# Gate and up tiles of a feed-forward in pairs by seven quarter products, with five feed-forward parts

## The chip, the cores and the metric

The kernel runs on one core of one Trainium2 chip. The metric is the device time of one execution in microseconds (us). Three runs of the kernel before gave 2639.88, 2640.99 and 2644.07 us, a median of 2640.99 us.

## The reference

One inference step of a two-layer hybrid trunk (width 1024) for 128 prompt tokens and 512 sample tokens, which share the weights. Each layer computes

```
h = rmsnorm(x) * (1 + scale1) + shift1
z = h @ w_in                        # conv, attention and S5 inputs, three gates
merged = sum_i sigmoid(g_i) * (y_i @ w_proj_i)
x += gate1 * (merged @ w_out)
h = rmsnorm(x) * (1 + scale2) + shift2
x += gate2 * ((silu(h @ w_ffn_gate) * (h @ w_ffn_up)) @ w_ffn_down)
```

The feed-forward width is 2816. All inputs are float32, and the result is compared at float32 accuracy.

## The kernel before

Channels lie on the 128 partitions and all 640 tokens along the free axis, so one pass over the weights serves both groups. Every operand of a large product is split exactly into two float32r parts (`split`, L255: ACT writes hi, DVE subtracts and writes lo), and a product is three matmuls: hi*hi, hi*lo, lo*hi. `gemm` (L732) computes one output tile of 128 channels by 640 tokens: for each of 8 blocks of 128 input channels, three products of two token halves of 320 columns, 48 matmuls in a PSUM tile of two banks. PSUM holds four such tiles (`bps`, L190; `gps` holds one until `release`).

Weights come as a stream of 512 KB blocks in the fixed order of a list (`order`, L284): SP issues a load into a ring of 3 buffers (`w_load`, L365); `converter` (L376) splits a block into one of 3 `wh` buffers, at most two blocks ahead of use. A feed-forward gate or up tile takes one block.

The order of the instructions on each engine is made when the program is built. The main products are a generator (`layer`, L1667); other work (attention, S5, weight conversion) are generators too (`Side`, L405), and `pump` (L431) emits a piece of side work when an estimated clock (`Clock`, L58) says that it can start before the next main product. The estimates set the order alone.

The feed-forward of a layer goes in two halves of 11 channel tiles. For each tile: the gate product (`fg`), tanh on ACT, a product on DVE, the up product (`fu`), a product on DVE and a split. Then 8 down products (`fd`) of 66 matmuls each, which read the 11 split tiles; `gated` (L751) adds each of them to the residual stream by three DVE operations. Before the down products of the second half of layer 0, the S5 preparation of layer 1 is started as side work. In layer 0 a block of the modulation products (`ada`, 8 short matmuls) follows many tiles.

At the start of the feed-forward, `norm` (L660) makes the 8 normalized blocks one after another, and `pair_gemm` (L767) runs the first gate and up tile side by side on them.

Semaphore waits are put in by the framework, by tile: a write to a tile waits for the reads of that tile emitted before it.

Of the kernel before, what the change touches and what calls it, by code (L numbers as in the profile page):

```python
# [14 lines left out]
D = 1024  # L15
# [29 lines left out]
NTILES = 57  # L45
RES = 1
FF_HALF = KF // 2
FD_ROWS = (((0, 6), (6, 5)), ((11, 6), (17, 5)))
# [62 lines left out]
class Engine:  # L111
    """forwards instructions to an engine and notes them in the clock"""
# [4 lines left out]
    def __getattr__(self, op):  # L117
# [11 lines left out]
        def call(*args, **kw):  # L129
# [38 lines left out]
def trunk_kernel(ctx: ExitStack, tc: tile.TileContext, a):  # L168
# [9 lines left out]
    whp = ctx.enter_context(tc.tile_pool(name="whp", bufs=3))  # L178
# [11 lines left out]
    def bps():  # L190
        while clk.slot("m") >= clk.HELD:
            min((x for x in sides if not x.busy), key=lambda x: x.time()).step()
# [62 lines left out]
    def split(x):  # L255
        """x = hi + lo exactly, both representable as float32r"""
# [5 lines left out]
    def split4(x):  # L262
        """x / 4 in the same way, from and to a tile of tokens"""
# [20 lines left out]
    order = []  # L284

    def wblk(key, src, r0, nr, c0, ncol):
        order.append((key, src[r0 * 128:(r0 + nr) * 128, c0:c0 + ncol], nr, ncol))
# [14 lines left out]
    def ada_gap(n):  # L302
        """blocks of the modulation products for times at which TensorE would wait"""
# [3 lines left out]
    def ada_n(key):  # L307
        """blocks of the modulation products after a tile"""
# [3 lines left out]
        return int(nm == "o" and m < 7 - GO or l == 0 and (nm in ("cc", "cb") or nm == "fg" and m > 1 or nm == "fu" and m > 19))  # L312
# [5 lines left out]
    for l in range(DEPTH):  # L318
# [33 lines left out]
        for half in range(2):  # L352
            for m in range(FF_HALF * half, FF_HALF * half + FF_HALF):
                tblk(("fg", l, m), a["w_ffn_gate"][l], 0, KD, 128 * m, 128)
                tblk(("fu", l, m), a["w_ffn_up"][l], 0, KD, 128 * m, 128)
            for m in range(KD):
                for r0, nr in FD_ROWS[half]:
                    wblk(("fd", l, m, r0), a["w_ffn_down"][l], r0, nr, 128 * m, 128)
# [3 lines left out]
    wst = {"load": 0, "use": 0, "pair": 0}  # L362
    wraw, wtile = {}, {}

    def w_load():  # L365
# [3 lines left out]
        key, src, nr, ncol = order[i]  # L369
        t = wrp.tile([128, 1024], F32, tag="wr", name="wr")  # L370
        clk.ring("wr", t.name, WR)
        sp.dma_start(t[:, :nr * ncol].rearrange("p (k m) -> p k m", k=nr), src.rearrange("(k p) m -> p k m", p=128))
        wraw[i] = t
        wst["load"] += 1

    def converter():  # L376
        for i, (key, src, nr, ncol) in enumerate(order):
            yield lambda: i in wraw and i < wst["use"] + 2 - wst["pair"]
            if key[0] == "ada":
                wtile[i] = wraw.pop(i)[:, :nr * ncol].rearrange("p (k m) -> p k m", k=nr)  # L380
                continue
            yield wraw[i], "act", "wh"
            t = wraw.pop(i)
            hl = whp.tile([128, 2, 1024], F32R, tag="wh", name="wh")
            clk.ring("wh", hl.name, 3)
            n = nr * ncol
            act.copy(hl[:, 0, :n], t[:, :n])
            yield hl, "dve"
            sub(hl[:, 1, :n], t[:, :n], f32(hl[:, 0, :n]))
            wtile[i] = [hl[:, r, :n].rearrange("p (k m) -> p k m", k=nr) for r in range(2)]  # L390
            w_load()

    def w_get(key):
        i = wst["use"]
        assert order[i][0] == key, (order[i][0], key)
        wst["use"] += 1
        while i not in wtile:
            cvt.step()
        return wtile.pop(i)

# [4 lines left out]
    class Side:  # L405
        """work beside the main products: a generator that yields, before each piece, what the first instruction
        of the piece needs (see Clock.ready), or a condition to wait for"""

        def __init__(self, gen, prio):
            self.gen, self.prio, self.done, self.busy = gen, prio, False, False  # L410
# [20 lines left out]
    def pump(need=(), until=None):  # L431
        """emits the side work that can start before the main products"""
        own = [x for x in need if isinstance(x, str) and x in clk.t]
        m = clk.ready(need)
        while until is None or not until.done:
# [4 lines left out]
            t, x = min(((x.time(), x) for x in sides if not x.busy and (x.prio < 0 or not clk.calm)), key=lambda y: y[0], default=(INF, None))  # L440
# [44 lines left out]
    # conditions between zeros: a window puts them on the rows of a slot  # L485
# [1430 lines left out]
```

## Time and profile before

| | us |
|---|---|
| three runs | 2639.88, 2640.99, 2644.07 |
| median | 2640.99 |
| span of the profiled execution | 2643.2 |
| TensorE busy | 2554.0 (97%) |
| VectorE (DVE) busy | 1580.0 (60%) |
| ScalarE (ACT) busy | 1016.2 (38%) |
| GpSimd (POOL) busy | 0.2 (0%) |

The page gives the span (from the first to the last instruction) of the profiled execution; its own time is one of the order of the three runs, between 2639.88 and 2644.07. The kernel is bound by TensorE almost throughout: what counts is the number of matmuls, the pace at which they start, and the stretches in which TensorE waits. Busy time of the other engines matters only where TensorE, or something on its way, waits for them. In the views, PE is TensorE, DVE VectorE, SPq the queue of SyncE that issues loads; `c` are tiles of tokens, `wh` split weights, `wr` raw weights, `bps` PSUM tiles, `pt` buffers that the attention uses for probabilities.

### The profile page before, as it was taken

What the parts mean: (1) busy time and instruction counts of PE and PEld (TensorE: products, weight loads), DVE (VectorE), ACT (ScalarE), POOL (GpSimd) and SP (SyncE); (2) the same over time, 40 slices, a digit from 0 to 9 for tenths busy, and PEclk for the clock granted to TensorE, in tenths of its full rate; (3) what the DMA queues carried; (4) which work ended last, traced back from release to release, by engine and by line L of the source; (5) the groups of instructions that cost most, each with busy time, mean ns of one, the idle gap of its engine ahead of it and who ended that gap; (6) DMA issues with size and microseconds to landing.
All of it is one profiled execution on the core that took longest, in us unless ns stands there. A gap on an engine that the chain in (4) does not pass through costs nothing. (4 is left out here: it accounts for less than half of the span.)

```text
span 2643.2 us, 44920 instructions
## 1 busy us (share of the span) xinstructions
PE 2554.0 (97%) x18683; PEld 2460.0 (93%) x18683; DVE 1580.0 (60%) x2982; ACT 1016.2 (38%) x1835; POOL 0.2 (0%) x4
## 2 busy tenths in 40 slices
PE   6999999999899999999989999999998999999998
PEld 4899999999888999999989999989998989999998
DVE  5888887788744433233677897578776453333333
ACT  4334336566622421122253333466664242212222
POOL 0000000000000000000000000000000000000000
PEclk8999999999999999999989999999999999999999
DMA  9433321121057233333334233212211633223222
GB/s 266 133 110 110 110 76 54 60 69 41 9 168 215 75 110 88 88 112 105 89 119 113 66 112 102 74 51 69 59 41 56 206 113 88 62 75 88 72 63 73
DMA packets 404411, 250.53 MB, mean 95 GB/s; under 512 B 57768, under 2 KB 392432, under 8 KB 404208
## 3 DMA queue, kind: packets, MB, share of 16 engines
q1 hardware_dynamic: 404208, 247.66, 31.9%
q8 instruction: 147, 2.41, 0.4%
q14 instruction: 56, 0.46, 0.1%
HBM read 227.49 MB, written 20.12 MB: 94 GB/s over the span
## 5 line engine op out<-in xcount | busy, mean ns | idle before, releaser
L130 PE MATMUL bps<-c,wh 128*128 128x320 f32 x12672 | 1952.1, 312 | 37.9 <-ACT c L130 18.4
L130 PEld LDWEIGHTS bps<-c,wh 128*128 128x128 f32 x12672 | 1876.4, 189 | 75.9 <-issue 25.1
L130 DVE TENSOR_TENSOR wh<-wr,wh 128x1024 fp32r<-128x1024 f32 (+2 forms) x308 | 353.8, 1153 | 223.6 <-ACT wh L130 213.8
L130 DVE TENSOR_TENSOR c<-c,c 128x512 f32<-128x512 f32 (+10 forms) x722 | 407.5, 590 | 71.6 <-ACT c L130 62.1
L130 ACT CAST wh<-wr 128x1024 fp32r<-128x1024 f32 (+2 forms) x308 | 303.7, 990 | 318.1 <-PE bps L130 177.9
L130 DVE SCALAR_TENSOR_TENSOR c<-c,bps 128x640 f32<-128x640 f32 (+1 forms) x108 | 83.2, 771 | 245.9 <-ACT c L130 169.6
L130 ACT CAST c<-c 128x640 fp32r<-128x640 f32 (+3 forms) x172 | 102.3, 621 | 327.0 <-DVE c L130 322.4
L130 DVE TENSOR_TENSOR c<-c,bps 128x640 f32<-128x640 f32 (+1 forms) x108 | 82.8, 769 | 205.9 <-PE bps L130 202.6
L130 PE MATMUL bps<-wh,c 128*128 128x256 f32 x1440 | 181.0, 284 | 2.0 <-ACT c L130 1.8
L130 ACT ACTIVATE c<-bps 128x640 f32<-128x640 f32 (+1 forms) x108 | 71.7, 664 | 285.3 <-PE bps L130 274.7
L130 PE MATMUL bps<-ident,c 128*128 128x128 f32 (+1 forms) x1115 | 159.1, 280 | 19.6 <-DVE c L130 7.4
L130 PEld LDWEIGHTS bps<-wh,c 128*128 128x128 f32 x1440 | 175.4, 191 | 2.7 <-ACT c L130 2.2
L130 PE MATMUL bps<-c,c 128*128 128x320 f32 (+2 forms) x960 | 159.5, 297 | 8.3 <-ACT c L130 4.5
L130 PEld LDWEIGHTS bps<-ident,c 128*128 128x128 f32 (+1 forms) x1115 | 132.6, 145 | 30.2 <-issue 8.9
L130 PEld LDWEIGHTS bps<-c,c 128*128 128x128 f32 x960 | 134.3, 191 | 13.4 <-ACT c L130 9.6
L130 ACT COPY c<-bps 64x256 f32<-64x256 f32 (+7 forms) x210 | 85.5, 445 | 155.8 <-PE bps L130 154.3
L130 ACT ACTIVATE c<-c 128x640 f32<-128x640 f32 (+4 forms) x93 | 65.3, 716 | 206.7 <-DVE c L130 206.5
L130 ACT ACTIVATE c<-bps,mx 128x640 f32<-128x640 f32 (+1 forms) x160 | 113.3, 713 | 36.1 <-DVE mx L130 35.6
L130 DVE TENSOR_REDUCE mx<-bps 128x1 f32<-128x640 f32 (+1 forms) x136 | 109.6, 809 | 26.4 <-PE bps L130 26.1
L130 DVE TENSOR_TENSOR pt<-bps,pt 128x640 fp32r<-128x640 f32 (+1 forms) x136 | 109.1, 810 | 15.3 <-ACT pt L130 14.5
L130 ACT CAST pt<-bps 128x640 fp32r<-128x640 f32 (+1 forms) x136 | 92.3, 687 | 26.6 <-PE bps L130 25.7
L130 PE MATMUL bps<-pt,c 128*128 128x256 f32 (+1 forms) x656 | 96.0, 292 | 2.9 <-DVE pt L130 2.1
(98 smaller groups left out, 1072.7 us busy)
## 6 DMA issues: line engine op xcount, KB each, us to landing
wr<-in_w_in_dram SPq DMA_DIRECT2D x104, 512.0 KB
wr<-in_w_ada_dram SPq DMA_DIRECT2D x62, 512.0 KB
wr<-in_w_ffn_gate_dram SPq DMA_DIRECT2D x44, 512.0 KB
wr<-in_w_ffn_up_dram SPq DMA_DIRECT2D x44, 512.0 KB
c<-in_w_ada_dram SPq DMA_DIRECT2D x68, 256.0 KB
wr<-in_w_ffn_down_dram SPq DMA_DIRECT2D x32, 384.0 KB
wr<-in_w_ffn_down_dram SPq DMA_DIRECT2D x32, 320.0 KB
wr<-in_w_proj_attn_dram SPq DMA_DIRECT2D x16, 512.0 KB
```

Source lines behind the costliest of these rows:

```text
L130: res = f(*args, **kw)
```

## The change

Of the 22 feed-forward channel tiles of a layer, the first three stay as they were. For the other 19, gate and up tile are computed together. The input channels are cut in two halves and the tokens in two halves of 320; the sums of input quarters (`sums`, `quarters`) and of weight quarters are made beforehand, and seven products of quarters take the place of eight. A quarter product (`quarter`) is 4 blocks by 3 products, 12 matmuls of 320 columns. The combined weights need three raw blocks: `wpair` loads gate weights, and up weights twice; onto half of each of two of them a DMA from GpSimd's queue adds gate or up weights from DRAM (`accum_op=OP.add`), and DVE adds two 512-word pieces. So a pair converts 3.5 blocks (before: 2), in a fixed order inside the pair (`advance`, with `cvt.hold`). `glu_pair` holds two PSUM tiles X and Y and uses their banks 0 and 1 in the order X0, X1, X0, Y1, X0, Y1, Y0; ACT copies partial results out and DVE adds them. The activation and split of a pair (`rest`) are emitted in the next pair, or before the down products.

The feed-forward goes in five parts of 4, 4, 4, 5 and 5 tiles, each followed by 8 down products of 24 or 30 matmuls. There are 4 `wh` buffers (one serves the attention's tables as `A.room`), 54 token tiles in place of 57, and the estimated cost of a float32r matmul is 32 columns larger.

```diff
+FF_PARTS = ((0, 4), (4, 4), (8, 4), (12, 5), (17, 5))
+PLAIN = 3
...
-                    cost = max(n, 256) / 2.4
+                    cost = (max(n, 256) + 32) / 2.4
...
+    def wpair(key, src1, src2, c0):
+        x, y = src1[0:D, c0:c0 + 128], src2[0:D, c0:c0 + 128]
+        order.append((key + (0,), [(0, x, None)], 8, 128))
+        order.append((key + (1,), [(512, y[0:512], x[0:512])], 4, 128))
+        order.append((key + (2,), [(0, y, y[512:1024])], 8, 128))
...
+        for o, x, y in srcs:
+            sp.dma_start(*rows(o, x))
+            if y is not None:
+                pool.dma_start(*rows(o, y), accum_op=OP.add)
...
+    def quarter(ps, b, w, i, xs, first, last=True):
+        K = len(xs)
+        for k, x in enumerate(xs):
+            yield (w[0],) + x + (() if k else (ps,))
+            for n, (r, s) in enumerate(((0, 0), (0, 1), (1, 0))):
+                mm(ps[:, b, 0:HN], w[r][:, K * i + k, :], x[s], first and k == 0 and n == 0, k == K - 1 and n == 2)
...
+    def glu_pair(l, m, x, hid, tail):
+        key = ("fgu", l, m)
+        half = lambda t: (t[:, 0:HN], t[:, HN:])
+        X = gps()
+        w = w_get(key + (0,))
+        advance(1)
+        next(tail)
+        yield from quarter(X, 0, w, 0, x["b11"], True)
+        p = c2()
+        c1, v = half(p)
+        act.copy(c1, X[:, 0, 0:HN])
+        next(tail)
+        advance(9)
+        yield from quarter(X, 1, w, 1, x["b21"], True)
+        w = w_get(key + (1,))
+        next(tail)
+        advance(1)
+        g = c2()
+        add(g[:, 0:HN], c1, X[:, 1, 0:HN])
+        next(tail, None)
+        yield from quarter(X, 0, w, 0, x["t2"], False)
+        act.copy(v, X[:, 0, 0:HN])
+        advance(9)
+        Y = gps()
+        yield from quarter(Y, 1, w, 1, x["t3"], True)
+        r = c2()
+        b, c7 = half(r)
+        act.copy(c7, Y[:, 1, 0:HN])
+        w = w_get(key + (2,))
+        advance(1)
+        yield from quarter(X, 0, w, 0, x["t1"], False)
+        act.copy(b, X[:, 0, 0:HN])
+        e = c2()
+        add(e[:, HN:], c7, X[:, 0, 0:HN])
+        release(X)
+        advance(9)
+        yield from quarter(Y, 1, w, 1, x["t4"], False)
+        add(e[:, 0:HN], v, Y[:, 1, 0:HN])
+        w = w_get(key + (3,))
+        advance(1)
+        advance(9)
+        yield from quarter(Y, 0, w, 0, x["b22"], True)
+
+        def rest():
+            add(g[:, HN:], b, Y[:, 0, 0:HN])
+            release(Y)
+            act.activation(p, g, AF.Tanh, scale=0.5)
+            yield
+            stt(g, p, 1.0, g, OP.add, OP.mult)
+            stt(g, g, -1.0, e, OP.mult, OP.mult)
+            yield
+            hi, lo = c2(F32R), c2(F32R)
+            act.copy(hi, g)
+            yield
+            sub(lo, g, f32(hi))
+            hid.append((hi, lo))
```

On PE, in a gate or up tile of layer 1, before (`c2` are split inputs, `wh` split weights, `bps` the PSUM tile): a new tile begins, and its waits are for weights and for a free PSUM tile.

```order
L130 MATMUL bps_23244<-c2_22485,wh_23135 128x320 x2
L130 MATMUL bps_23304<-c2_22429,wh_23201 128x320 [waits DVE_49,Activation_49]
L130 MATMUL bps_23304<-c2_22429,wh_23201 128x320
L130 MATMUL bps_23304<-c2_22430,wh_23201 128x320 x2
L130 MATMUL bps_23304<-c2_22429,wh_23201 128x320 [waits DVE_49]
```

On PE in a pair of layer 1 now: the end of the first quarter product (bank 0 of `bps_24611`, which is X) and the start of the second one (bank 1 of the same tile).

```order
L132 MATMUL bps_24611<-c2_22866,wh_24530 128x320
L132 MATMUL bps_24611<-c2_22882,wh_24530 128x320
L132 MATMUL bps_24611<-c2_22883,wh_24530 128x320
L132 MATMUL bps_24611<-c2_22882,wh_24530 128x320
L132 MATMUL bps_24611<-c2_22842,wh_24530 128x320 [waits Activation_49]
L132 MATMUL bps_24611<-c2_22843,wh_24530 128x320
```

The second quarter product now begins with a wait for ACT; the value waited for is reached by ACT's copy of bank 0 into `c2_24628`, which itself waits for the last matmul of the first quarter product. In the same way the third one (X, bank 0) waits for DVE's sum out of bank 1 of X, and the seventh one (Y, bank 0) for DVE's sum out of bank 1 of Y.

On DVE in that pair, from the fifth to the seventh quarter product and on into the next pair (`c2_24701` takes the sums of the up side, `c2_24652` those of the gate side):

```order
L132 TENSOR_TENSOR c2_24701<-c2_24684,bps_24611 128x320 [waits Activation_49]
L132 TENSOR_TENSOR wh_24686<-pt_24376,wh_24686 128x1024 [waits DMASW4_49,PE_49]
L132 TENSOR_TENSOR c2_24701<-c2_24628,bps_24671 128x320 [waits PE_49]
L132 TENSOR_TENSOR wh_24717<-pt_24379,wh_24717 128x1024 [waits Activation_49]
L132 TENSOR_TENSOR c2_24652<-c2_24684,bps_24671 128x320 [waits PE_49]
L132 SCALAR_TENSOR_TENSOR c2_24652<-c2_24628,c2_24652 128x640 [waits Activation_49]
```

The sum out of Y's bank 1 (third row), for which the seventh quarter product waits, stands behind the sum out of X and a weight conversion of 1024 words.

On DVE at the start of the feed-forward of layer 1, before: the last split of an input block, and then the conversion of the next gate tile's weights (`wh_22572`).

```order
L130 TENSOR_TENSOR c2_22486<-c2_22482,c2_22485 128x640 [waits DVE_49,Activation_49]
L130 TENSOR_TENSOR wh_22572<-wr_22285,wh_22572 128x1024 [waits DMAHW2_49,Activation_49]
L130 SCALAR_TENSOR_TENSOR c2_22491<-c2_22491,bps_22492 128x640 [waits Activation_49]
L130 TENSOR_TENSOR c2_22491<-c2_22491,bps_22493 128x640 [waits DVE_49,PE_49]
L130 TENSOR_TENSOR c2_22599<-c2_22491,c2_22598 128x640 [waits Activation_49]
```

And now, at the same place (`wh_22973` are that tile's weights):

```order
L132 TENSOR_TENSOR c2_22891<-c2_22887,c2_22890 128x640 [waits DVE_49,Activation_49]
L132 TENSOR_TENSOR c2_22896<-c2_22832 128x320
L132 SCALAR_TENSOR_TENSOR c2_22981<-c2_22839,c2_22896 128x320 [waits DVE_49]
L132 TENSOR_TENSOR c2_22897<-c2_22839,c2_22832 128x320
L132 SCALAR_TENSOR_TENSOR c2_22981<-c2_22981,c2_22839 128x320 [waits DVE_49]
L132 SCALAR_TENSOR_TENSOR c2_22898<-c2_22898,bps_22899 128x640 [waits Activation_49]
L132 TENSOR_TENSOR c2_22898<-c2_22898,bps_22900 128x640 [waits DVE_49,PE_49]
L132 TENSOR_TENSOR c2_23008<-c2_22898,c2_23007 128x640 [waits DMAHW2_49,Activation_49]
L132 TENSOR_TENSOR wh_22973<-wr_22671,wh_22973 128x1024 [waits DMAHW5_49]
```

The conversion moved from the second place to behind four input sums and the whole evacuation of the first tile. The order in layer 0 is the same.

## Rows read from the trace of the kernel before

**Rows 1.** The page's first part: span; busy time of each engine, share, instructions.

```profile
span 2643.2 us, 44920 instructions
PE 2554.0 (97%) x18683; PEld 2460.0 (93%) x18683; DVE 1580.0 (60%) x2982; ACT 1016.2 (38%) x1835; POOL 0.2 (0%) x4
```

**Rows 2.** Busy time by stretch, feed-forward of layer 1 (columns in the first line).

```profile
core 0: us, PE busy (x) PEld busy (x) DVE busy (x) ACT busy (x) POOL busy (x), PEclk, DMA share, GB/s
2250.00:2300.00 50.00, 50.00 (x343) 50.00 (x342) 16.80 (x17) 11.59 (x14) 0.00 (x0) 1.00 0.24 69
```

**Rows 3.** Groups by operation and shape: count, busy us, mean ns, idle before.

```profile
L130 PE MATMUL bps<-c,wh 128*128 128x320 f32 x2544 | 379.6, 310 | 0.9 <-ACT c L130 0.6 <-DVE c L130 0.3
...
L130 PE MATMUL bps<-wr,csT 128*32 128x256 f32 x496 | 39.2, 391 | 0.0
```

**Rows 4.** The same view for ACT and DVE, whole span.

```profile
L130 ACT CAST wh<-wr 128x1024 fp32r<-128x1024 f32 x244 | 254.5, 1046 | 196.0 <-DMA wr<-in_w_proj_attn_dram 78.8 <-PE bps L130 77.0 <-DMA wr<-in_w_out_dram 32.5
L130 ACT CAST c<-c 128x640 fp32r<-128x640 f32 x116 | 81.8, 727 | 327.0 <-DVE c L130 322.4 <-issue 3.6
L130 ACT ACTIVATE c<-bps 128x320 f32<-128x320 f32 x16 | 7.0, 436 | 23.0 <-PE bps L130 15.7 <-issue 7.3
...
L130 DVE TENSOR_TENSOR wh<-wr,wh 128x1024 fp32r<-128x1024 f32 x244 | 297.5, 1222 | 141.0 <-ACT wh L130 131.3
L130 DVE SCALAR_TENSOR_TENSOR c<-c,bps 128x640 f32<-128x640 f32 x92 | 75.5, 821 | 245.1 <-ACT c L130 168.8 <-PE bps L130 75.9
L130 DVE TENSOR_TENSOR c<-c,bps 128x320 f32<-128x320 f32 x16 | 7.7, 482 | 2.8 <-ACT c L130 2.8
```

**Rows 5.** Timeline, hand-overs between engines: start, length, engine, operation, [idle before].

```profile
2007.88 0.74 PE L130 MATMUL bps<-ident,c 128*128 128x128 f32 x5 [1.10 <-DVE pt L130]
2008.66 0.69 ACT L130 CAST pt<-bps 128x640 fp32r<-128x640 f32 x1 [0.74 <-PE bps L130]
...
2160.09 0.82 DVE L130 TENSOR_TENSOR c<-c,c 128x640 fp32r<-128x640 f32 x1 [1.29 <-ACT c L130]
2160.11 0.56 PE L130 MATMUL bps<-c,wh 128*128 128x320 f32 x2 [1.47 <-ACT c L130]
2160.97 4.29 PE L130 MATMUL bps<-c,wh 128*128 128x320 f32 x26 [0.30 <-DVE c L130]
...
2310.28 0.82 DVE L130 SCALAR_TENSOR_TENSOR c<-c,bps 128x640 f32<-128x640 f32 x1 [4.47 <-ACT c L130]
2311.01 0.82 DVE L130 TENSOR_TENSOR wh<-wr,wh 128x640 fp32r<-128x640 f32 x1
```

**Rows 6.** Timeline, DVE and ACT at the start of layer 1's feed-forward.

```profile
2174.08 1.23 DVE L130 TENSOR_TENSOR wh<-wr,wh 128x1024 fp32r<-128x1024 f32 x1
2174.90 0.70 ACT L130 ACTIVATE c<-bps 128x640 f32<-128x640 f32 x1 [0.85 <-PE bps L130]
2175.64 0.82 DVE L130 SCALAR_TENSOR_TENSOR c<-c,bps 128x640 f32<-128x640 f32 x1 [0.33 <-ACT c L130]
...
2178.17 0.83 DVE L130 TENSOR_TENSOR c<-c,c 128x640 fp32r<-128x640 f32 x1 [0.79 <-ACT c L130]
```

**Rows 7.** Timeline of PE, waits around the end of layer 0.

```profile
1290.35 29.31 PE L130 MATMUL bps<-c,wh 128*128 128x320 f32 x198 [1.77 <-DVE wh L130]
...
1361.60 2.47 PE L130 MATMUL bps<-c,ones 128*128 128x320 f32 x4 [3.21 <-DVE c L130]
```

**Rows 8.** Busy time by stretch around the same waits (columns as in rows 2).

```profile
1300.00:1330.00 30.00, 28.26 (x193) 28.00 (x192) 28.83 (x106) 7.93 (x17) 0.00 (x0) 1.00 0.25 73
...
1360.00:1390.00 30.00, 26.34 (x179) 23.78 (x180) 19.48 (x27) 22.62 (x39) 0.00 (x0) 0.82 0.41 145
```

**Rows 9.** Timeline, a 512 KB weight load and the conversion that waited for it.

```profile
2107.82 0.37 SPq L130 DMA_DIRECT2D wr<-in_w_out_dram  x1
...
2112.85 1.05 ACT L130 CAST wh<-wr 128x1024 fp32r<-128x1024 f32 x1 [2.11 <-DMA wr<-in_w_out_dram]
```

More of the change, by code (lines that the diff above doesn't have):

```diff
@@ L191, in bps @@
         while clk.slot("m") >= clk.HELD:
-            min((x for x in sides if not x.busy), key=lambda x: x.time()).step()
+            min((x for x in sides if not x.busy and not x.hold), key=lambda x: x.time()).step()
         t = psb.tile([128, 2, 512], F32, tag="b", name="bps")
@@ L368, in w_load @@
             return
[L369 to L372, printed above, removed]
+        key, srcs, nr, ncol = order[i]
+        part = key[0] == "fgu" and key[3]
+        if part:
+            t = f32(ptp.tile([128, 2, TK], F32R, tag="pt", name="pt").rearrange("p a b -> p (a b)"))
+        else:
+            t = wrp.tile([128, 1024], F32, tag="wr", name="wr")
+            clk.ring("wr", t.name, WR)
@@ L373, in w_load @@
+        rows = lambda o, x: (t[:, o:o + x.shape[0] // 128 * ncol].rearrange("p (k m) -> p k m", m=ncol),
+                             x.rearrange("(k p) m -> p k m", p=128))
+        for o, x, y in srcs:
+            sp.dma_start(*rows(o, x))
+            if y is not None:
+                pool.dma_start(*rows(o, y), accum_op=OP.add)
         wraw[i] = t
         wst["load"] += 1
-    def converter():
-        for i, (key, src, nr, ncol) in enumerate(order):
-            yield lambda: i in wraw and i < wst["use"] + 2 - wst["pair"]
-            if key[0] == "ada":
[L380 to L391, printed above, removed]
+        if key[0] == "fgu" and key[3] < 2:
+            w_load()
@@ new lines, in wh_tile, with may, halves @@
+    def wh_tile():
+        hl = whp.tile([128, 2, 1024], F32R, tag="wh", name="wh")
+        clk.ring("wh", hl.name, WH)
+        return hl
+    def may():
+        return wst["made"] < wst["used"] + wst["deep"] - wst["pair"]
+    def halves(t, n):
+        yield t, "act", "wh"
+        hl = wh_tile()
+        wst["made"] += 1
+        act.copy(hl[:, 0, :n], t[:, :n])
+        yield hl, "dve"
+        sub(hl[:, 1, :n], t[:, :n], f32(hl[:, 0, :n]))
+        return [hl[:, r, :n] for r in range(2)]
@@ L396, in w_get, with advance @@
         wst["use"] += 1
-        while i not in wtile:
+        if key[0] != "ada":
+            wst["used"] += 1
+        while u not in wtile:
             cvt.step()
-        return wtile.pop(i)
+        return wtile.pop(u)
+    def advance(n):
+        while n and not cvt.done:
+            if callable(cvt.need):
+                if not cvt.need():
+                    return
+            else:
+                n -= 1
+            cvt.step()
     sides = []
@@ L439, in pump @@
                 m = max(clk.ready(need), clk.t["pe"])
-            t, x = min(((x.time(), x) for x in sides if not x.busy and (x.prio < 0 or not clk.calm)), key=lambda y: y[0], default=(INF, None))
+            t, x = min(((x.time(), x) for x in sides if not x.busy and not x.hold and (x.prio < 0 or not clk.calm)), key=lambda y: y[0], default=(INF, None))
             if t > m + SLACK or x is None or own and t == m and x.prio >= 0:
@@ L729, in reload_x, with gemm @@
         return xs
[L732 removed]
+    def gemm(ps, w, c0, acts, first=True, last=True, ks=None):
         K = len(acts)
[L735 removed]
+        for i, k in enumerate(ks or range(K)):
             x = acts[k]
[L737 removed]
+            if last and i >= K - RES:
                 clk.spare = 1
[L739 removed]
+            yield (w[0],) + x + (() if i else (ps,))
             for n, (r, s) in enumerate(((0, 0), (0, 1), (1, 0))):
@@ new lines, in glu_pair @@
+    def glu_pair(l, m, x, hid, tail):
[53 more added lines that the diff above has]
+            hid.append((hi, lo))
+        for _ in range(ada_n(key)):
+            yield from ada_step()
+        return rest()
@@ L1761, in layer @@
                 yield from tile_gemm(("fu", l, m), hs, ev_u)
-            if not half:
+            advance(9)
+            for _ in tail:
+                pass
+            cvt.hold = False
+            final = m0 + nm == KF
+            if not final:
                 ada_flush(l, 5)
```

190 lines of the change are left out of this document (141 added, 49 removed).

## The prediction

> **What bounds the kernel now.** I read the page's first part first: TensorE is busy 97% of the span, the next engine 60% [rows 1]. So a change pays by matmuls left out and costs by stops of TensorE; work of other engines counts only where TensorE waits for it. Then the stretch that the change rewrites: in 50 us of gate and up tiles TensorE is busy all 50.00 us with 343 matmuls of 320 columns, while DVE has 16.80 and ACT 11.59 us of work, and the DMA share is 0.24 [rows 2]. There is not one stop, and the pace is 50/343 = 145.8 ns per matmul. A single matmul is recorded with 310 ns [rows 3]: starts are 146 ns apart, so after the last start TensorE's result is complete some 0.164 us later than the pace alone says. That is nothing while matmuls follow each other, and is paid whenever somebody must see the result before TensorE goes on. The third thing to read is what a hand-over costs, from places where TensorE does wait [rows 5]: a block of transposes ends at 2007.88 + 0.74 = 2008.62 and ACT begins at 2008.66 (0.04 us); a restart of two matmuls takes 0.56 us where 0.146 + 0.310 = 0.456 would do (0.10 us more); DVE's split ends at 2160.91 and TensorE goes on at 2160.97 (0.06 us). Consecutive DVE operations overlap by 0.09 us (2310.28 + 0.82 against 2311.01).
>
> **What is removed.** A pair had 96 matmuls and has 84. 38 pairs (19 in each layer) save 38 x 12 = 456, at 145.8 ns: **-66.5 us**. The down products have as many matmuls as before (66 x 16 = 24 x 24 + 30 x 16 = 1056 in each layer).
>
> **What is added inside a pair.** The seven products use two PSUM tiles of two banks each, in the order X0, X1, X0, Y1, X0, Y1, Y0, and a write to a tile waits for the reads of that tile which stand ahead of it. So a write to one bank waits for the reading of the other, and three of these reads begin only when the product just issued is complete. Nothing else stands ready for TensorE there. From the durations of ACT's copy of 128x320 out of PSUM (0.436) and of DVE's sum of the same size (0.482) [rows 4]:
>
> (a) second product waits for ACT's copy after the first: 0.164 + 0.04 + 0.436 + 0.06 + 0.10 = 0.80 us; 38 times 30.4 us.
>
> (b) third product waits for DVE's sum after the second: 0.164 + 0.04 + 0.482 + 0.06 + 0.10 = 0.85; 38 times 32.3 us.
>
> (c) seventh product waits for DVE's sum after the sixth. On DVE that stands behind the sum after the fifth, which waits for ACT's copy, and behind a weight subtraction of 1024 words (1.222 [rows 4]). From the end of the fifth product: 0.164 + 0.04 + 0.436 + 0.06 + 0.482 + 1.222 + 0.482 + 0.06 + 0.10 = 3.05, less two overlaps of 0.09 = 2.87. The sixth product covers 12 x 0.146 = 1.75, so 1.12 us are left, in 28 pairs. In the 10 last pairs of a part the subtraction has 512 words, and DVE is free when the sixth product ends: 0.85 as in (b). Together 28 x 1.12 + 10 x 0.85 = 39.9 us.
>
> The fifth and sixth products wait for ACT's copies that the product before them covers: 0. So a pair takes 12.25 + 2.77 = 15.0 us, where two tiles took 96 x 0.146 = 14.0 before: more than the 12 matmuls are worth.
>
> ACT's conversions (3.5 a pair of 1.046 us, four copies, tanh, a cast) come to 6.8 us, DVE's (3.5 x 1.222, sums, products, the splits) to some 10 us of those 15: covered. In the first pair of each layer ACT's first copy stands behind casts of the input splits; I take three of the 0.727 us casts [rows 4] as uncovered, 2.2 us, in each layer: **+4.4**.
>
> **Loads.** A pair moves 1.75 MB where it moved 1.0; in 15 us that is 117 GB/s, and the kernel runs at 145 GB/s with a DMA share of 0.41 elsewhere [rows 8]. A 512 KB load is issued at 2107.82 and its conversion starts at 2112.85, so 5.0 us at most [rows 9]. The trace has no accumulating DMA. From below it costs what half such a load does, 2.5 us; from above I double the 5.0. Two stand in GpSimd's queue per pair, each waiting for the load under it; they decide only if one takes over 15.0/2 = 7.5 us. I take 5, hidden by the loads that run more than a pair ahead: 0. By the Trainium skill ("DMA: Bandwidth & Descriptors", section "Anatomy of one DMA") a DMA from GpSimd takes about 2.0 us and 436 KB per us more, an estimate of 2.6 us for 256 KB; no run here shows it, and the sum would be the same.
>
> **Ends of parts.** The last pair of a part has no next pair to hide its end: sum 0.482, tanh 0.70, two products of 0.82, cast 0.73 [rows 4, 6] make 3.55, with drain and hand-overs about 4.0 us, and the split's lo half (0.82) is late by some 0.7 more. The down products can run over the other tiles first: 3 x 2 x 3 = 18 matmuls = 2.62 us (parts of four) or 24 = 3.5 us (of five). That leaves 2.08 us three times and 1.2 twice, 8.65 in a layer, 17.3 in both; in layer 0 `ada` blocks of 8 matmuls (8 x 39.2/496 = 0.63 us [rows 3]) stand in some of the gaps, which I count as -3.4: **+13.9**. The five evacuations of the residual, in place of two, lie beside matmuls: 0. The S5 preparation before layer 1 gets 8 x 30 matmuls = 35 us of cover in place of 77; its places in the order are about the same: 0, between -6 and +10.
>
> **Start of the feed-forward.** Before, DVE subtracts the next gate tile's weights at 2174.08 and TensorE never waits [rows 6]. Now this stands behind four sums of inputs and the whole evacuation of the first tile. The last split ends at 2179.0 [rows 6]; pushing the evacuation and the subtraction behind it brings the lo weights to about 2179.0 + 1.23 + 0.06 = 2180.3, while TensorE wants them at some 2176.1 (ACT reads the gate tile at 2174.90 [rows 6], so the last gate matmul was paced out at 2174.90 - 0.04 - 0.164 = 2174.70; then come 6 matmuls of the up tile and 4 with the hi weights, 1.46 us): 4.2 us, twice = 8.4. A stop of 3.21 us is followed by a granted clock of 0.82 over 30 us, while behind one of 1.77 us it stays at 1.00 [rows 7, 8]; 18% of 30 us is at most 5.4 us lost. I add half of it, 2.5 a layer: **+13.4**.
>
> **Sum.** -66.5 + 102.6 + 4.4 + 13.9 + 13.4 = +67.8 us. The profiled execution (span 2643.2, own time between 2639.88 and 2644.07) lies within 0.15% of the median 2640.99, so 2641 + 68 = **2709 us**. Bounds: if each wait costs just the reader's length (1.40 a pair, 53.2), half the ends and no clock, -66.5 + 53.2 + 7 + 8.4 = +2: 2643. If restarts cost 0.20, DVE operations don't overlap (3.45 a pair, 131), the clock loses 5.4 each time and S5 10: -66.5 + 131 + 4.4 + 13.9 + 19.2 + 10 = +112: 2753.
>
> **Rivals.**
>
> 1. *The waits are met without a stop, faster.* The writes go to another bank than the read that they wait for. If what they wait for is reached earlier than I read it, only the ends and the start remain: -66.5 + 27.3 = -39, **2602 us**. It decides where the three waits of a pair sum to less than (66.5 - 27.3)/38 = 1.03 us. Against it: the built order shows a wait at each of these matmuls, and the readers' lengths alone make 1.40. The Trainium skill ("PSUM — Partial Sum Buffer", section "PSUM bank collisions raise a hardware error") asks for guards by bank and quadrant; under that rule alone these writes would need no wait. The order has them nevertheless, and no row of this trace shows two banks of a tile used apart. Chance 0.08.
>
> 2. *Only the readers count.* Drain, hand-over and restart lie beside the reading: the lower bound, **2643 us**, no difference. The 1.10 us stop in [rows 5] speaks against it, as it holds hand-overs too. Chance 0.05.
>
> 3. *The accumulating DMAs bound.* At 10 us each, a pair takes 20 us: +5 x 38 = 190 more, **2899 us**; 7.5 us is the point. For it: all go through one queue in order. Against: half the bytes of a load that takes 5.0. The Trainium skill ("SBUF — State Buffer", section "SBUF: two separate sides") says that a DMA of GpSimd's queue can be held up while DVE runs some SBUF-only operations; that would put it here, and GpSimd has no work in this trace that could show it. Chance 0.05.
>
> 4. *The clock falls inside pairs.* TensorE would be busy only 12.25/15.0 = 82% there. At the lower level a pair's 84 matmuls take up to 12.25 us more; in one pair of four that is 9.5 x 12.25 = 116, **2825 us**. Against it: stops of about 0.8 to 1.1 us, shorter than the 1.77 after which the clock stayed at 1.00 [rows 7, 8]. Chance 0.05.
>
> **The numbers.** My forecast has 0.77. 0.2% (5 us) is about what a measurement of this kernel tells from no change. Faster: rival 1 and a little of the forecast's spread, 0.09; the same: rival 2, 0.05; slower: 0.86. The range runs from the lower bound, which takes in rival 2, to the upper one: 2643 to 2756. Rivals 1, 3 and 4 (0.18) are left out.
>
> **What would show it.** The matmuls of split operands must fall from 12672 to 12216. In a stretch of pairs TensorE should stop three times a pair, once for ACT and twice for DVE, for 0.8 to 1.1 us each, and a pair should take 15.0 us. There should be a stop of about 4 us at the start of each feed-forward, and 1 to 2 us before the down products of each part. Conversions should not wait for the accumulated weights. I am wrong if the stops in pairs are absent or near 0.4 us, if a pair takes 14 us or less, if weights are late, or if the granted clock is 0.5 in stretches of pairs.

## The result, and the profile after

The changed kernel took 2814.32 us (median of 4 runs, 2812.13 to 2817.54) against 2640.43 us (4 runs, 2638.23 to 2644.07) for the kernel before: a ratio of 1.0657, with a 95% interval of 1.0642 to 1.0672. It is slower, as forecast, but by 174 us where the forecast had 68, and 58 us above the upper end of its range.

The page of the changed kernel, its first part and its group of main products:

```profile
span 2814.3 us, 45358 instructions
...
PE 2568.2 (91%) x18235; PEld 2424.0 (86%) x18235; DVE 1837.2 (65%) x3491; ACT 1164.2 (41%) x2107; POOL 98.0 (3%) x80
...
L132 PE MATMUL bps<-c,wh 128*128 128x320 f32 x12216 | 1947.2, 316 | 160.0 <-DVE c L132 99.9
```

The count fell by 456, to 12216. Yet TensorE's busy time rose by 14 us against [rows 1], since each stop adds a drain and a restart (0.27 us, worked out below) and matmuls behind the long stops of layer 0 run at a lower clock (0.94 in the second stretch below, 1.00 before). Its idle time went from 89 to 246 us. To see where, the span is cut in four at the first matmul with `ones` of a normalization (the first layer up to its feed-forward, that feed-forward, the second layer up to its own, the rest). Busy time by stretch, of the kernel before and of the changed one; the columns are those of [rows 2]:

```profile
0.00:848.39 848.39, 804.44 (x6074) 760.85 (x6074) 622.13 (x1268) 390.24 (x765) 0.20 (x4) 0.98 0.37 109
848.39:1354.54 506.15, 498.66 (x3527) 478.55 (x3525) 218.58 (x406) 126.96 (x181) 0.00 (x0) 1.00 0.33 95
1354.54:2148.52 793.98, 766.66 (x5763) 741.39 (x5763) 561.34 (x1064) 372.78 (x724) 0.00 (x0) 0.98 0.31 93
2148.52:2643.20 494.68, 484.28 (x3326) 479.20 (x3324) 177.99 (x244) 126.24 (x165) 0.00 (x0) 0.99 0.25 72
```

```profile
0.00:864.92 864.92, 810.04 (x6073) 758.92 (x6074) 620.67 (x1262) 394.46 (x771) 0.20 (x4) 0.98 0.36 108
864.92:1463.32 598.40, 503.71 (x3258) 464.64 (x3257) 317.94 (x554) 192.65 (x294) 48.97 (x38) 0.94 0.46 106
1463.32:2276.78 813.46, 775.56 (x5810) 745.00 (x5811) 591.25 (x1174) 379.19 (x745) 0.00 (x0) 0.98 0.30 91
2276.78:2814.30 537.52, 478.88 (x3098) 455.44 (x3096) 307.34 (x502) 197.93 (x297) 48.79 (x38) 0.97 0.42 93
```

The differences are +16.5, +92.3, +19.5 and +42.8 us, 171.1 in all. The two feed-forwards have the same work but for the modulation blocks and the S5 preparation of layer 1, and layer 0's loses 50 us more; 36 us went where the diff changes no product at all.

TensorE's timeline in layer 1's feed-forward (start, length, operation, idle before):

```profile
2310.02 31.13 PE L132 MATMUL bps<-c,wh 128*128 128x320 f32 x200 [3.86 <-DVE wh L132]
2343.39 2.83 PE L132 MATMUL bps<-c,wh 128*128 128x320 f32 x12 [2.25 <-ACT c L132]
...
2393.54 2.02 PE L132 MATMUL bps<-c,wh 128*128 128x320 f32 x12 [0.52 <-ACT c L132]
2396.21 7.30 PE L132 MATMUL bps<-c,wh 128*128 128x320 f32 x48 [0.65 <-DVE c L132]
2404.32 3.79 PE L132 MATMUL bps<-c,wh 128*128 128x320 f32 x24 [0.81 <-DVE c L132]
2408.63 2.02 PE L132 MATMUL bps<-c,wh 128*128 128x320 f32 x12 [0.52 <-ACT c L132]
...
2449.34 4.66 PE L132 MATMUL bps<-c,wh 128*128 128x320 f32 x30 [0.58 <-DVE c L132]
2455.25 0.56 PE L132 MATMUL bps<-c,wh 128*128 128x320 f32 x2 [1.25 <-ACT c L132]
2456.11 4.23 PE L132 MATMUL bps<-c,wh 128*128 128x320 f32 x17 [0.30 <-DVE c L132]
```

This is the forecast's picture: three stops a pair, once for ACT and twice for DVE, before the second, third and seventh product; from one second product to the next 2408.63 - 2393.54 = 15.09 us. The first row is the stop at the start, the second that of the first pair, the last two the end of a part.

In layer 0 the third stop of a pair is another one. All engines from the end of one pair to the seventh product of the next:

```profile
982.78 0.37 SPq L132 DMA_DIRECT2D wr<-in_w_ada_dram  x1
...
993.27 0.64 PE L132 MATMUL bps<-wr,csT 128*32 128x256 f32 x8
...
993.97 0.37 SPq L132 DMA_DIRECT2D wr<-in_w_ffn_gate_dram  x1
994.43 1.08 SPq L132 DMA_DIRECT2D pt<-in_w_ffn_up_dram  x2
...
999.35 1.28 POOL L132 DMA_DIRECT2D pt<-in_w_ffn_gate_dram  x1 [22.03 <-DVE c L132]
1001.45 1.28 POOL L132 DMA_DIRECT2D pt<-in_w_ffn_up_dram  x1 [0.82 <-DMA pt<-in_w_ffn_up_dram]
1006.35 0.69 DVE L132 TENSOR_TENSOR pt<-pt,wr 128x512 f32<-128x512 f32 x1 [5.50 <-DMA pt<-in_w_ffn_up_dram]
...
1007.12 1.04 ACT L132 CAST wh<-pt 128x1024 fp32r<-128x1024 f32 x1 [3.83 <-DVE pt L132]
1008.08 0.42 ACT L132 COPY c<-bps 128x320 f32<-128x320 f32 x1
1008.53 0.49 DVE L132 TENSOR_TENSOR c<-c,bps 128x320 f32<-128x320 f32 x1 [0.76 <-ACT c L132]
...
1010.07 0.48 DVE L132 TENSOR_TENSOR c<-c,bps 128x320 f32<-128x320 f32 x1
...
1010.60 3.57 PE L132 MATMUL bps<-c,wh 128*128 128x320 f32 x12 [4.26 <-DVE c L132]
```

SyncE issues the load of a modulation block at 982.78 and the next load, which is the next pair's, only at 993.97, when the modulation product of 993.27 has ended. On top of these bases GpSimd issues the two accumulating transfers at 999.35 and, when the second base has landed, at 1001.45; the weight sum that needs them starts at 1006.35, 12.4 us after the first load. DVE waits 5.50 us for them, ACT's conversion behind that sum 3.83 us, and behind these, in order, stand the copy (1008.08) and the sum (1008.53) out of X, and then the sum out of Y (1010.07) for which this pair's own seventh product waits. TensorE stops for 4.26 us, and the next 12 matmuls take 3.57 us in place of 2.02.

### The profile page after: what moved, and what is told of

The parts are those of the page before. It is cut to its first block, busy times and chain, and to the rows that moved or that the text cites. A ratio compares the mean times of both kernels' runs of the same rounds, so it can differ in the third digit from the quotient of the medians.

```text
span 2814.3 us, 45358 instructions
## 1 busy us (share of the span) xinstructions
PE 2568.2 (91%) x18235; PEld 2424.0 (86%) x18235; DVE 1837.2 (65%) x3491; ACT 1164.2 (41%) x2107; POOL 98.0 (3%) x80
## 5 line engine op out<-in xcount | busy, mean ns | idle before, releaser
L132 PEld LDWEIGHTS bps<-c,wh 128*128 128x128 f32 x12216 | 1836.3, 192 | 232.8 <-DVE c L132 128.0
L132 DVE TENSOR_TENSOR wh<-wr,wh 128x1024 fp32r<-128x1024 f32 (+2 forms) x324 | 335.5, 1039 | 162.9 <-ACT wh L132 162.3
L132 DVE TENSOR_TENSOR c<-c,c 128x512 f32<-128x512 f32 (+7 forms) x666 | 393.3, 614 | 66.6 <-ACT c L132 57.2
L132 DVE TENSOR_TENSOR c<-c,bps 128x320 f32<-128x320 f32 (+1 forms) x222 | 125.4, 566 | 214.9 <-ACT c L132 115.0
L132 ACT COPY c<-bps 128x320 f32<-128x320 f32 (+8 forms) x363 | 151.0, 437 | 273.8 <-PE bps L132 270.7
L132 ACT ACTIVATE c<-c 128x640 f32<-128x640 f32 (+4 forms) x131 | 93.5, 722 | 191.0 <-DVE c L132 190.5
L132 PEld LDWEIGHTS bps<-c,c 128*128 128x128 f32 x960 | 135.4, 193 | 19.5 <-ACT c L132 14.9
L132 DVE SCALAR_TENSOR_TENSOR c<-bps,g2T,c 128x128 f32<-128x128 f32 (+2 forms) x240 | 90.5, 433 | 81.6 <-PE bps L132 81.6
L132 POOL DMA_DIRECT2D pt<-in_w_ffn_gate_dram x38 | 48.9, 1288 | 2583.6 <-DVE c L132 2090.5
L132 DVE SCALAR_TENSOR_TENSOR c<-c,c 128x640 f32<-128x640 f32 (+3 forms) x124 | 102.8, 836 | 48.1 <-ACT c L132 46.2
L132 ACT CAST wh<-pt 128x1024 fp32r<-128x1024 f32 x76 | 79.0, 1047 | 120.4 <-DVE pt L132 91.8
```

The source lines that it names most:

```text
L132: res = f(*args, **kw)
```

## The experiments

Where no number of runs is given, a time is that of one run; the kernel before took 2639.1, 2639.6 and 2643.9 us beside the three sets of runs. The times of the four stretches, cut in the same way, in us (each to within 0.1; the sum is the span). Some expectations cut elsewhere: those of e1 and e3 at the first product on normalized blocks (876.7 where the table has 864.9), that of e9 leaves out the first 32 us.

| run | first layer | feed-forward 0 | second layer | feed-forward 1 |
|---|---|---|---|---|
| before | 848.4 | 506.1 | 794.0 | 494.7 |
| changed | 864.9 | 598.4 | 813.5 | 537.5 |
| e1_own_tiles | 865.2 | 527.5 | 815.1 | 478.4 |
| e2_ada_moved | 864.6 | 595.8 | 824.0 | 535.2 |
| e6_ada_other_buffers | 864.8 | 538.9 | 818.9 | 533.8 |
| e3_estimate | 859.0 | 594.2 | 805.7 | 533.3 |
| e4_before_estimate | 869.9 | 513.9 | 813.6 | 494.4 |
| e9_before_8 | 857.5 | 510.7 | 796.2 | 494.6 |
| e5_before_55 | 844.7 | 505.9 | 798.1 | 495.9 |
| e7_sums_later | 868.3 | 598.2 | 813.7 | 533.8 |
| e10_start | 866.6 | 592.0 | 813.3 | 530.7 |
| e8_all | 858.0 | 482.2 | 800.9 | 479.9 |
| e11_all_start | 864.3 | 474.9 | 802.4 | 474.6 |
| e12_all_outside | 872.2 | 477.3 | 799.4 | 476.2 |

How far can a single stretch be trusted? In the first and the second layer e3, e8 and e11 hold the same operations in the same order, and so do e1, e6, e7 and e10. They still differ by up to 6.3 us in one stretch (858.0 to 864.3 and 813.3 to 818.9), so a smaller difference of one stretch is not to be read by itself.

### The stops inside a pair

```diff
-        yield from quarter(X, 1, w, 1, x["b21"], True)
+        X1 = twin(X)
+        yield from quarter(X1, 1, w, 1, x["b21"], True)
...
-        add(g[:, 0:HN], c1, X[:, 1, 0:HN])
+        add(g[:, 0:HN], c1, X1[:, 1, 0:HN])
...
-        yield from quarter(Y, 0, w, 0, x["b22"], True)
+        Y0 = twin(Y)
+        yield from quarter(Y0, 0, w, 0, x["b22"], True)
...
-            add(g[:, HN:], b, Y[:, 0, 0:HN])
+            add(g[:, HN:], b, Y0[:, 0, 0:HN])
```

`twin` takes another PSUM tile that the estimated clock counts as the first one, so that the order stays.

> The second product of a pair gets a PSUM tile of its own, and the seventh one too; the order of the instructions on every engine stays as in the changed kernel. Theory (the stops in a pair come from two banks that share one tile): in layer 1 the three stops of 0.52, 0.65 and 0.81 us vanish, a pair goes from 15.09 to about 12.3 us, and the feed-forward of layer 1 (from the first matmul on normalized blocks to the end) from 523.5 to about 470 us. In layer 0 some of the gain is eaten by weights that come late already, so the whole is 2814 - 53 - (10 to 53) = 2708 to 2751 us. Rival (the same instructions wait for the same engines a little later, since ACT and DVE work in order): a pair stays above 14 us and the whole above 2780 us.

Measured: 2688.21 us, 126 less, and 20 below the lower end of what was expected. Busy time in a stretch of layer 1's pairs, and TensorE's timeline there:

```profile
2320.00:2360.00 40.00, 40.00 (x275) 40.00 (x274) 27.71 (x39) 21.00 (x33) 3.87 (x3) 1.00 0.43 85
```

```profile
2309.79 55.90 PE L133 MATMUL bps<-c,wh 128*128 128x320 f32 x380
2366.93 0.56 PE L133 MATMUL bps<-c,wh 128*128 128x320 f32 x2 [1.25 <-ACT c L133]
```

380 matmuls follow each other without a stop, at 40.00/275 = 145.5 ns: a pair of 84 takes 12.2 us. Feed-forward 1 went from 537.5 to 478.4, below the 494.7 of before. Layer 0 gained 71, more than the 53 at most that I gave it. I read it so: the seventh product, with a tile of its own, no longer waits for a sum that stands behind late weights; it wasn't tried by itself. The rows of layer 0 fit: the ten stops of 3.7 to 7.4 us before seventh products are gone, and six stops of 1.7 to 3.0 us stand before the first product of a next pair instead. TensorE's idle time in that stretch goes from 94.7 to 43.6 us.

### The late weights of layer 0

First the modulation blocks were moved behind down products:

```diff
-            return int(l == 0 and m > 1) + int(l == 0 and m > 19)
+            return int(l == 0 and m == PLAIN)
+        if nm == "fd":
+            return int(l == 0 and m in FD_ADA.get(key[3], ()))
```

with `FD_ADA = {0: range(0, 5), 4: range(0, 5), 8: range(0, 5), 12: range(0, 5)}`, and an `ada_step` for each behind `release(ps)` of a down product. The loads of the blocks move with them (`tblk` in place of `wblk` for the weights of down products).

> Twenty of the modulation blocks of layer 0 stand after down products of the first four parts instead of after the pairs. Theory (behind the 4 us stops of layer 0 is the order of the loads: a modulation block takes one of three raw buffers and a place in the queue, the next pair's loads are issued only when it has been used, and conversions that wait for them hold DVE and ACT): the stops of 3.7 to 7.4 us before the seventh products of layer 0 fall to 0.8, the feed-forward of layer 0 goes from 594 to about 535 us, the whole to 2750 us (2735 to 2770). Rival (the accumulating transfers are too slow by themselves, 4.7 us from issue to landing and two in a row, or the memory is busy): the stops stay and the whole is over 2800 us.

Measured: 2821.60 us, no gain. TensorE's timeline in the second part of layer 0:

```profile
996.67 3.57 PE L133 MATMUL bps<-c,wh 128*128 128x320 f32 x12 [6.50 <-ACT c L133]
1000.82 9.74 PE L133 MATMUL bps<-c,wh 128*128 128x320 f32 x48 [0.58 <-DVE c L133]
1011.38 3.79 PE L133 MATMUL bps<-c,wh 128*128 128x320 f32 x24 [0.81 <-DVE c L133]
```

By the time it is a miss, and I could not call the theory right by it. The rows tell more: the stops of the later pairs did fall to 0.81 us, and one of 6.5 us came at the first pair of a part, whose loads now stand behind modulation blocks. The delay had moved with the blocks: TensorE is idle for 89.5 us in this stretch, and for 94.7 in the changed kernel. So the next run left the blocks at their places and took only their buffers out of the ring:

```diff
-                    ada_blk(ada_n(("fgu", l, m)))
+                    ada_gap(ada_n(("fgu", l, m)))
...
         key = ("fgu", l, m)
+        ada_pre(ada_n(key))
...
-        for _ in range(ada_n(key)):
-            yield from ada_step()
+        ada_fill(ada_n(key))
```

> The modulation blocks of layer 0's pairs stay after their pairs, but are loaded at the start of the pair into token tiles, not into the ring of three raw buffers. Theory (the ring makes the next pair's loads wait for the modulation block): the stops of 3.7 to 7.4 us in layer 0 fall to 0.8 us, the second and later pairs of a part take 15.1 us and the short matmuls, the stretch of layer 0's feed-forward goes from 598 to about 545 us and the whole to 2760 us (2750 to 2775). Rival (accumulating transfers too slow, memory busy): the stops stay, 2814 us.

Measured: 2758.37 us, with 538.9 us in feed-forward 0 (545 expected).

```profile
996.23 2.02 PE L132 MATMUL bps<-c,wh 128*128 128x320 f32 x12 [0.52 <-ACT c L132]
998.90 7.30 PE L132 MATMUL bps<-c,wh 128*128 128x320 f32 x48 [0.65 <-DVE c L132]
1007.01 2.02 PE L132 MATMUL bps<-c,wh 128*128 128x320 f32 x12 [0.81 <-DVE c L132]
1008.96 0.64 PE L132 MATMUL bps<-c,csT 128*32 128x256 f32 x8
1009.53 2.02 PE L132 MATMUL bps<-c,wh 128*128 128x320 f32 x12
1012.07 2.02 PE L132 MATMUL bps<-c,wh 128*128 128x320 f32 x12 [0.52 <-ACT c L132]
```

The stop before the seventh product is 0.81 us, a pair with its modulation block takes 1012.07 - 996.23 = 15.84 us, as in layer 1 and the block. The accumulating transfers are all still there; only what the loads under them stand behind has changed. The two loads under them and the weight sum for the same pair as in the rows of the changed kernel:

```profile
978.82 2.54 SPq L132 DMA_DIRECT2D pt<-in_w_ffn_up_dram  x2
...
1000.63 0.68 DVE L132 TENSOR_TENSOR pt<-pt,wr 128x512 f32<-128x512 f32 x1
```

The loads are issued from 978.82 instead of 994.43, and the sum waits for nothing, though an accumulating transfer takes some 7 us in this feed-forward (the median of 38) and 4.8 in the changed kernel's. So it is the late start of the loads, and not the length of the transfers. This run takes the blocks out of the ring and also issues their loads earlier. That the buffer is what counts is shown by the changed kernel: between 983 and 1016 us SyncE's queue waits for TensorE twice, 28.5 us together, and the only raw buffers that TensorE reads are those with a modulation block.

### The 36 us outside the feed-forwards

The estimated cost of a float32r matmul only sets the order of side work. It was made smaller in the changed kernel, then larger in the kernel before:

```diff
-                    cost = (max(n, 256) + 32) / 2.4
+                    cost = (max(n, 256) + 8) / 2.4
```

> The changed kernel with an estimated cost of a float32r matmul that is 8 columns larger than before instead of 32 (the estimate sets the order of side work alone). Theory (the 36 us that were lost outside the two feed-forwards come from the order that the larger estimate gives): the stretch up to the feed-forward of layer 0 goes from 876.7 back to about 861 us and the one between the feed-forwards from 819.9 to about 800 us, the whole to about 2778 us. Rival (they come from 54 token tiles and the tables in a weight buffer): both stretches stay, and the whole at 2814 us.

Measured: 2794.18 us; the two outer stretches took 859.0 and 805.7. The direction is the theory's, the size not: 14 of 36 us. The two runs of all parts below have the same order outside, and with them the outer stretches take 1658.9 to 1666.7 us together, where five runs with 32 columns (the changed kernel, e1, e6, e7, e10) take 1678.4 to 1683.7 and the kernel before 1642.4. So 8 columns give back 12 to 25 us and leave 16 to 24. The changed kernel with the estimate of before was not run.

```diff
-                    cost = max(n, 256) / 2.4
+                    cost = (max(n, 256) + 24) / 2.4
```

> The kernel before with an estimate that is 24 columns larger, nothing else. Theory (the estimate costs 36 us outside the feed-forwards): 2641 + some 20 to 36 = 2661 to 2677 us. Rival (token tiles and tables): 2641 us, with the stretch up to the feed-forward of layer 0 at 861 us.

Measured: 2693.54 us, 54 above before and 17 above the theory's range, though nothing but this number changed: 869.9 and 813.6 us outside, against 864.9 and 813.5 in the changed kernel, and 8 us more in feed-forward 0. In the first stretch TensorE is idle for 869.93 - 814.09 = 55.8 us where it was 44.0, and recorded as busy 9.7 us longer:

```profile
0.00:869.93 869.93, 814.09 (x6074) 763.66 (x6075) 622.16 (x1265) 393.63 (x768) 0.20 (x4) 0.98 0.36 107
1383.81:2197.44 813.63, 776.65 (x5716) 748.30 (x5715) 553.04 (x1050) 379.24 (x730) 0.00 (x0) 0.97 0.30 90
```

What the estimate of 8 columns had left could be the smaller number of token tiles (`NTILES = 55` in place of 57, two of the three that the changed kernel lacks), or 8 columns themselves:

> The kernel before with 55 token tiles in place of 57, nothing else. Theory (of the 36 us that the changed kernel lost outside the feed-forwards, what an estimate of 8 columns leaves, some 22 us, is the shortage of token tiles): 2641 + 10 to 25 us, in the stretches up to the feed-forward of layer 0 and between the feed-forwards. Rival (it is the remaining estimate): 2641 us within 5.

Measured: 2646.33 us, just outside what the rival was given (2641 within 5) and below the theory's 2651; it is 6.7 us above before beside it. But the two outer stretches together are only 0.4 us longer. So two token tiles less cost next to nothing there.

> The kernel before with an estimate 8 columns larger, nothing else. Theory (the estimate alone explains what is lost outside the feed-forwards; 8 columns gave 827.4 and 805.7 us in the changed kernel where the kernel before has 816.5 and 794.0): the same two stretches take about 827 and 806 us, the whole 2641 + 22 = 2663 us. Rival (8 columns are harmless, and the rest is due to the tables in a weight buffer or the fourth buffer): 2641 us within 6.

Measured: 2660.75 us (2663 expected), with 857.5 and 796.2 us outside. The total agrees by luck: the outer stretches lost 11 us where 22 were expected, feed-forward 0 lost another 5, and before took 2643.9 in this set, not 2641. The first stretch is about what the changed kernel has with the same estimate (858.0 to 864.3 in three runs), the second falls short of it by 4.7 to 9.5 us. That remainder is open; the tables in a weight buffer and the fourth buffer were not tried alone.

### The start of a feed-forward

```diff
-        side = Side(sums(hp, tt_), -0.3)
...
                     yield from pair_gemm(("fg", l, m), ("fu", l, m), hs, ev_g, ev_u, KS)
+                    side = Side(sums(hp, tt_), -0.3)
```

> The sums of input blocks are started only after the first gate and up tile, so that the second gate tile's weights are converted at the place where they stood before. Theory (the stop of 3.86 us at the start of each feed-forward is that conversion's place on DVE, and costs some 2 us of lower clock more): both stops go, the whole to 2814 - 12 = 2802 us (2798 to 2806). Rival (the sums are then late for the first pair): a stop of the same length comes at the first pair, 2814 us or more.

Measured: 2815.95 us: the rival. The stop of 3.86 us went, and the first pair's grew from 2.25 to 3.20 us in layer 1, and to 6.55 us in layer 0. Layer 1's in TensorE's timeline, and what DVE waits for ahead of layer 0's:

```profile
2294.26 44.70 PE L132 MATMUL bps<-c,wh 128*128 128x320 f32 x298 [0.30 <-DVE c L132]
2342.16 3.30 PE L132 MATMUL bps<-c,wh 128*128 128x320 f32 x11 [3.20 <-ACT c L132]
```

```profile
914.01 0.69 DVE L132 TENSOR_TENSOR pt<-pt,wr 128x512 f32<-128x512 f32 x1 [5.89 <-DMA pt<-in_w_ffn_up_dram]
```

A sum of weights waits 5.89 us for its transfer, and the input sums that come later in DVE's order wait with it. So these were held back as well (in `pair_units`):

```diff
+        yield lambda: not sumq or sumq[0].done
         yield r1, r2, r3, "dve"
```

> The changed kernel with the sums of input blocks started after the first gate and up tile, and the sums of the first pair's weights held back until the input sums are done. Theory (the stop at the start is the place of a conversion on DVE; when it went, the first pair stopped since its inputs' sums and splits stood behind weight sums that waited for their transfer): both stops fall, 2814 - 12 = 2802 us (2796 to 2806). Rival (the input sums, splits and conversions are simply too much work for 28 us): the first pair stops by 3 us or more again, 2812 us or more.

Measured: 2804.54 us, 10 less than the changed kernel and in the range. The stop at the start is gone in both layers; the first pair stops by 2.52 us in layer 0, and by 2.24 us in layer 1, as it did in the changed kernel:

```profile
2289.61 40.96 PE L132 MATMUL bps<-c,wh 128*128 128x320 f32 x274
2332.81 3.41 PE L132 MATMUL bps<-c,wh 128*128 128x320 f32 x12 [2.24 <-ACT c L132]
```

### Together

> Together: a PSUM tile of their own for the second and seventh products, modulation blocks in token tiles, sums later, and an estimate 8 columns larger than before in place of 32. Theory: the first stretch alone gave 2688; the loads of layer 0 give another 25 to 35, the head 10 to 12, the estimate 15 to 20: 2615 to 2640 us, so not slower than the kernel before (2640). Rival (the parts overlap, or pairs of 12.3 us run into their loads, 1.75 MB in a pair or 143 GB/s): 2655 to 2680 us.

Measured: 2627.13 us (4 runs), in the range; a ratio to before of 0.9954 (0.9937 to 0.9970). A first pair stops by 4.58 us in layer 0 and by 5.07 us in layer 1.

> The four parts together as in the run of all parts, with the first pair's weight sums held back as well. Theory: 2627 less two stops of 4.6 and 5.1 us at the first pairs and their lower clock, 2614 us (2608 to 2620). Rival: the stops stay, 2627 us.

Measured: 2617.62 us (4 runs), in the range; a ratio of 0.9907 (0.9890 to 0.9924), so 0.9% less than the kernel before and clear of the interval. The two stops at first pairs are gone, and the feed-forwards take 7.3 and 5.3 us less than in the run of all parts. A part of layer 0 in TensorE's timeline:

```profile
976.41 12.58 PE L133 MATMUL bps<-c,wh 128*128 128x320 f32 x84
988.92 0.64 PE L133 MATMUL bps<-c,csT 128*32 128x256 f32 x8
989.49 12.58 PE L133 MATMUL bps<-c,wh 128*128 128x320 f32 x84
```

A pair is one row of 84 matmuls now. The feed-forwards take 31 and 20 us less than before, and the two stretches outside them lose 24 us of that again.

> The same with an estimate that is 8 columns smaller than before outside the feed-forwards and 8 columns larger inside them. Theory (only the order outside pays for a larger estimate): the stretches outside go back from 826 and 801 us to about 816 and 794, the whole to 2598 us (2590 to 2610). Rival (a smaller estimate is as bad as a larger one): 2614 us or more.

Measured: 2626.56 us: the rival. The first stretch is 872.2 us, the longest of all runs, while the second (799.4) is no longer than with 8 columns (800.9, 802.4). So in the first layer a smaller estimate is as bad as a larger one. That the value of before is one that suits the order, and not a point on a slope, is my reading: it was not run with the pairs.

## Why the prediction was right and wrong

**What is removed**: right, 456 matmuls at 145.5 ns.

**Inside a pair**: right. Twelve matmuls between two stops are recorded with 2.02 us where the pace makes 1.75, so a stop costs 0.27 us more than its idle time: 0.79, 0.92 and 1.08 us (0.85 in the last pair of a part) against 0.80, 0.85 and 1.12 (0.85) in (a) to (c), and 15.09 us a pair against 15.0. The run with own tiles took them all away. Rival 1 asked for a sum under 1.03 us and rival 2 for 1.40, and it is 2.79. The Trainium skill ("PSUM — Partial Sum Buffer", section "PSUM bank collisions raise a hardware error") asks for guards by bank; the run with own tiles stands in for such a guard, and its rows agree: where the bank read and the bank written lie in different tiles, 380 matmuls pass without a stop. The guard in this kernel is by tile of two banks, and that is what cost.

**Ends of parts, first pairs, start**: right within a microsecond or so. The end of a part of four has stops of 1.25 and 0.30 us, with two times 0.27 a total of 2.1 (2.08 forecast); the first pair stops for 2.25 (3.0); the start for 3.86 (4.2), and the 200 matmuls behind it take 31.13 us at a granted clock of 0.95, 2.0 more than at pace (2.5). So feed-forward 1, for which the terms make -33.3 + 51.3 + 2.2 + 8.65 + 6.7 = +35.6, came out at +42.8.

**Loads**: wrong. The step was "hidden by the loads that run more than a pair ahead: 0". I had the length of an accumulating transfer about right (5 taken; medians of 4.6 and 4.8 us from issue to landing in the transfers of layer 0's second part, up to 6.8 in a part of layer 1's), and asked only whether the queue can keep the pace, 7.5 us for each. That it could: they overlap. But a late start costs too: from the first base to the sum that uses the transfers it is 12.4 us, and in layer 0 a modulation block between two pairs takes one of the three raw buffers, so that the loads of the next pair start when the block is used, and their conversions hold ACT and DVE for the pair that runs. I had looked at layer 1, where no such block is, and taken it for both. The prediction named this as a sign of being wrong ("if weights are late"). The late loads cost 598.4 - 538.9 = 59.5 us by the run with other buffers, 39 of them in TensorE's idle time and the rest in matmuls at a lower clock (0.94 over the stretch, 0.99 in that run). The estimate from the Trainium skill ("DMA: Bandwidth & Descriptors", section "Anatomy of one DMA"), 2.6 us for 256 KB, is short of the 4.6 us measured, and neither number would have shown the chain. Rival 3 had the place nearly, with another mechanism: not the bandwidth of the queue, the start.

**The estimate**: a term that the sum didn't have. The diff shows 32 columns more in a cost that only sets an order; I gave the stretches outside the feed-forwards no term for it; only the S5 preparation had a bound, 10 us. They lost 36 us; an estimate changed by itself in the kernel before lost 9 + 2 us with 8 columns and 21.5 + 19.6 with 24. So the estimate can cost as much; how much of the 36 us it did cost is shown for 12 to 25 only.

**Rival 4** fell: over one pair of layer 1 the granted clock is 1.00; in layer 0, where a pair has a stop of 4.26 us, it is 0.87. Columns as in [rows 2]:

```profile
2393.54:2408.63 15.09, 13.12 (x85) 12.33 (x85) 9.30 (x16) 6.02 (x9) 3.85 (x3) 1.00 0.71 152
993.84:1015.12 21.28, 15.86 (x97) 13.93 (x93) 9.66 (x14) 7.09 (x12) 2.56 (x2) 0.87 0.52 112
```

So of the 103 us (171.1 - 67.8) between forecast and result, 60 lie in layer 0's feed-forward and are the late loads, 36 lie outside the feed-forwards, of which the estimate gave 12 to 25 back, and 7 lie in layer 1's. Of these 7 about half may be scatter: two runs with the same operations there took 535.2 and 533.8 us in place of 537.5.

**The upper bound** holds a slip: with 0.10 more for each of three restarts and no overlap (2 x 0.09) a pair's waits come to 2.77 + 0.30 + 0.18 = 3.25 us, not 3.45, so the bound was 8 us too high. The measured time lies above it either way.

## What to carry to other kernels

Before a saving by fewer products is believed, follow each partial result's tile: where one tile holds two banks, a read of the one stops a write to the other, and here three such stops of 0.8 to 1.1 us cost 2.8 us in a pair that saved 1.75; a tile for each bank turned the loss in feed-forward 1 into a gain. Cover has a start as well as a rate: for each stage that has different neighbours in the same buffers, ask when the first transfer of a chain may be issued, not only whether the queue keeps up. And a number that sets an order is an edit like any other: give it a term with bounds, and try it alone.

## What the runs showed of the hardware that was not expected

An accumulating transfer of 256 KB took 4.8 us from issue to landing in layer 0's feed-forward and 6.4 in layer 1's (medians of 38; single ones 4.4 to 9.4), as long as or longer than a plain load of 512 KB (5.0 at most [rows 9]), and kept GpSimd busy for 1.28 us each. TensorE's clock stayed at its higher level (1.00) with three stops of 0.52 to 0.81 us in every 15 us, and was 0.87 on average where one of the stops was 4.26 us. The rows of the accumulating transfers in layer 0's second part (issue, size, median us to landing):

```profile
pt<-in_w_ffn_gate_dram POOLq DMA_DIRECT2D x2, 256.0 KB, 4.6
pt<-in_w_ffn_up_dram POOLq DMA_DIRECT2D x2, 256.0 KB, 4.8
```

They agree with the 5 us that the forecast took for one.
